# The RWKV-7 state update: old state added by identity products in PSUM, one scaling for each direction

## The chip, the cores and the metric

The kernel runs on one core of one Trainium2 chip. The metric is the device time of one execution in microseconds (us). Beside the timed executions, one execution was recorded by the hardware profiler; the profile's durations are those of that execution.

## The reference, cut to what matters

The model has two blocks. The change touches the first layer of the second block, whose core is a recurrence over tokens with a state of 64x64 for each of 12 heads, run once forward and once backward over 256 context tokens and 512 others:

```python
def rwkv7_scan(r, w, k, v, kk, bb, s0, reverse):
    def step(s, inp):
        r_t, w_t, k_t, v_t, kk_t, b_t = inp
        sa = jnp.einsum('bhij,bhj->bhi', s, kk_t)
        s = s * w_t[:, :, None, :] - sa[..., None] * b_t[:, :, None, :] + v_t[..., None] * k_t[:, :, None, :]
        return s, jnp.einsum('bhij,bhj->bhi', s, r_t)
    ...
    s, ys = lax.scan(step, s0, xs, reverse=reverse)
    return s, jnp.moveaxis(ys, 0, 1)
...
    for d in range(2):
        ...
        s_ctx, yc = rwkv7_scan(*tc[:6], zeros, d == 1)
        _, yl = rwkv7_scan(*tl[:6], s_ctx, d == 1)
```

Everything is in 32-bit floats. What comes before and after the recurrence (projections, gates, norms, the other layers and the whole first block) is the same before and after the change.

## The kernel before

**Chunks.** The kernel doesn't walk token by token. It cuts the 768 tokens into 12 chunks of 64, takes the heads in 6 pairs of two, and the chunks in 3 groups of 4. For each pair and group a good deal of work that doesn't depend on the state is done ahead: the decays and scaled keys (`inner_first`, called prep), the products between the tokens of a chunk (`products`, `keys_by_token`, called system), and the inverse of a triangular system for each chunk (`inner_rest`, `inner_second`, called inverse). What depends on the state is `Program.chain`, which runs 18 times (6 pairs by 3 groups), with 4 steps each. A step s handles chunk s of the forward direction (d = 0) and chunk 3-s of the backward one (d = 1).

**One step of the chain.** The state tile S has 128 partitions (two heads of 64), and 128 columns for each direction, in which the two heads stand as the diagonal 64x64 blocks; the other blocks are zero. S comes from a ring of five tiles that are zeroed once. In a step

- L1822 (two TensorE matmuls, one for each direction) adds WT times S to the PSUM tile u;
- the halves of u are copied, scaled, to VU: the forward half by ScalarE (the line in `chain` calls the helper `act`, so the profile shows it as L322), the backward half by VectorE (L1829);
- ScalarE scales the old state by the decay of the whole chunk, gs = gc * S, with two instructions of 128x128 (profile: L322, gs<-S,gc). The tile gs has one buffer, and EC, a tile of the inverse (L1763, written at L1765), has the same tag and so the same buffer;
- L1843 (four matmuls of 64x64, a head and a direction each) writes the step's new part to the PSUM tile sp, which has one buffer;
- L1851 (four VectorE instructions of 64x64) makes the new state: gc * sp + gs, block by block. At the first step of a pair there is no old state, and L1849 scales alone.

The last step of the last group has no update, so that 66 steps update the state, 60 of them with an old state. The new state is read by the next step's L1822 and, later, by the matmuls of L1864, which add its part to the outputs.

**What runs beside it.** `weave` (L1489) takes generators in turns: the chain of one group, the inverse of the next, the system of the one after that and the prep of the third, and, at a set rate, pieces of the projections (L363 to L365, three passes with weights and activations split in two parts; the profile calls their output acc). A `yield` in `chain` ends its turn. A scheduler orders the instructions of each engine when the program is built; an engine then runs its own list strictly in order, and semaphores hold it where an operand or a buffer isn't ready. TensorE's instructions of 32-bit operands appear in the trace as two passes for each matmul.

Of the kernel before, what the change touches and what calls it, by code (L numbers as in the profile page):

```python
# [11 lines left out]
F32 = mybir.dt.float32  # L12
F32R = mybir.dt.float32r
I32 = mybir.dt.int32
AF = mybir.ActivationFunctionType
ALU = mybir.AluOpType
PSUM = bass.MemoryType.PSUM

P = 128
# [254 lines left out]
class Program:  # L274
# [1013 lines left out]
    def rwkv(self, hl, hc):  # L1288
# [3 lines left out]
        with tc.tile_pool(name="rk", bufs=1) as rp:  # L1292
# [99 lines left out]
            inner = [{} for _ in range(nq)]  # L1392
            prep = lambda q: self.inner_first(q % 3, pairs[q // 3], inner[q]) if q < nq else iter(())
            system = lambda q: chain(self.products(q % 3, inner[q]), self.keys_by_token(inner[q])) if q < nq else iter(())
            inverse = lambda q: chain(self.inner_rest(q % 3, pairs[q // 3], inner[q]), self.inner_second(inner[q])) if q < nq else iter(())
            run(prep(0))
            run(system(0), prep(1))
# [3 lines left out]
            for q in range(nq):  # L1401
# [3 lines left out]
                if g == 0:  # L1405
                    if m:
                        feed.need((m - 1, "gate"))
                    run(self.pair_end(m - 1, pairs[m - 1]) if m else iter(()), system(q + 2), rate=RATE)
                    if m:
                        allow(m, "gate")  # L1410
                    start = ()
                    if m + 1 < NH2:
                        feed.need((m + 1, "v"))
                        start = self.pair_start(m + 1, pairs[m + 1])
                        feed.need((m + 1, "r"))
                    gens.append(chain(start, prep(q + 3)))
                else:
                    gens += [system(q + 2), prep(q + 3)]
# [273 lines left out]
    def inner_rest(self, g, pr, st):  # L1692
# [34 lines left out]
        for e in range(2):  # L1727
            H = half(1 - e)
            self.act(self.LB[H].rearrange("p (a j) t -> p a j t", j=2), st["system"](e))
        T = st["T"] = rp.tile([P, 8, 64], F32, tag="T", name="T")  # L1730
        for k in (1, 0):
            for e in range(2):
                H = half(1 - e)
                nc.sync.dma_start(out=T[H] if k else self.DB[H], in_=td[k, e::2, :4096].rearrange("u (s t) -> s u t", t=64))
        yield
# [5 lines left out]
    def inner_second(self, st):  # L1741
# [11 lines left out]
        def product(lhs, rhs, m=64, r0=0):  # L1753

            ps = self.psum("c", (P, 8, 32))
            for x in range(8):
                for i in (1, 0):
                    nc.tensor.matmul(ps[64 * i + r0:64 * i + r0 + m, x, :], lhs(x, half(i)), rhs(x, half(i)), start=True, stop=True)  # L1758
            return ps
# [3 lines left out]
        E, EC = self.E[0], rp.tile([P, 8, 32], F32, tag="gs", name="EC")  # L1763
        ps = product(lambda x, H: LB[H, x, :], lambda x, H: c16(Tm[H, x:x + 1], 0)[:, 0])
        tt(out=EC, in0=ps, in1=self.k_lmask.unsqueeze(1).to_broadcast([P, 8, 32]), op=ALU.mult)  # L1765
        self.act(c16(E, 0), b2(EC))
        yield
        ps = product(lambda x, H: Dm[H, x, :], lambda x, H: EC[H, x, :])
        tt(out=c16(Tm, 0), in0=c16(Tm, 0), in1=b2(ps), op=ALU.subtract)
# [28 lines left out]
    def chain(self, g, st, pr):  # L1798


        nc, rp = self.nc, self.rp
        tt = nc.vector.tensor_tensor
        half = lambda i: slice(64 * i, 64 * i + 64)
        Dm, VU, gc, M = self.DB, st["VU"], st["gc"], st["M"]
        if g == 0:
            self.state = None
            pr["y"] = rp.tile([P, 6, P], F32, tag="y", name="y")
        y = pr["y"]
        u = self.psum("u", (P, 2, 2, P))
        for d, h, j, e in self.units():  # L1810
            R = half(1 - e)
            nc.tensor.matmul(u[R, d, j, half(h)], Dm[R, 4 * d + 2 * h + j, :], st["akv"][R, 2 * d + h, j * 64:j * 64 + 64],
                             start=(d + h + j == 0), stop=True, skip_group_check=True)
        states = []
        for s in range(4):
            cs = (s, 3 - s)
            S = self.state
            states.append(S)
            if S is not None:
                for d in range(2):  # L1820
                    j, e = divmod(cs[d], 2)
                    nc.tensor.matmul(u[half(1 - e), d, j, :], st["WT"][:, d, j, half(1 - e)], S[:, d, :], start=False, stop=True, skip_group_check=True)  # L1822
            for d in range(2):
                j, e = divmod(cs[d], 2)
                O = half(1 - e)
                if d == 0:
                    self.act(VU[O, d, cs[d], :], u[O, d, j, :], scale=-0.5)
                else:
                    nc.vector.tensor_scalar(out=VU[O, d, cs[d], :], in0=u[O, d, j, :], scalar1=-0.5, scalar2=None, op0=ALU.mult)  # L1829
            if g == 2 and s == 3:  # L1830
                break
            nxt = self.S[self.turn % len(self.S)]
            self.turn += 1

            if S is not None:
                gs = rp.tile([P, 2, P], F32, tag="gs", name="gs")
                for d in range(2):
                    self.act(gs[:, d, :], S[:, d, :], AF.Copy, scale=gc[:, d, cs[d]:cs[d] + 1])
            yield
            sp = self.psum("sp", (P, 2, 64))  # L1840
            for d in range(2):
                for h in range(2):
                    nc.tensor.matmul(sp[half(h), d, :], st["bkT"][d][:, cs[d], half(h)], VU[:, d, cs[d], half(h)], start=True, stop=True)  # L1843
            for h in range(2):
                H = half(h)
                for d in range(2):
                    gd = gc[H, d, cs[d]:cs[d] + 1]
                    if S is None:
                        nc.vector.tensor_scalar(out=nxt[H, d, H], in0=sp[H, d], scalar1=gd, scalar2=None, op0=ALU.mult)  # L1849
                    else:  # L1850
                        nc.vector.scalar_tensor_tensor(out=nxt[H, d, H], in0=sp[H, d], scalar=gd, in1=gs[H, d, H], op0=ALU.mult, op1=ALU.add)  # L1851
            self.state = nxt
            yield
        yield
        ps = self.psum("misc", (P, 4, P))

        last = None
        for s, h, d in ((s, h, d) for s in range(4) for h in range(3) for d in (1, 0)):
            c = s if d == 0 else 3 - s
            X = half(c % 2)  # L1860
            if h < 2:
                ins = nc.tensor.matmul(ps[X, s, half(h)], M[:, d, h, c, half(1 - c % 2)], VU[:, d, c, half(h)], start=(s == 0 and h == 0), stop=True, skip_group_check=True)
            elif states[s] is not None:
                ins = nc.tensor.matmul(ps[X, s, :], st["AR"][d][:, c // 2, 3 - 3 * (c % 2), :], states[s][:, d, :], start=False, stop=True, skip_group_check=True)  # L1864
            else:
                continue
            last = self.queue(ins, last)
        for d in range(2):
            t0 = FIRST[g][d] // 2
            for e in range(2):  # L1870
                X = half(e)

                src = ps[X, e::2, :] if d == 0 else ps[X, (3 - e)::-2, :]
                dst = y[X, t0:t0 + 2, :]
                if g == 0:

                    i, s = (0, e) if d == 0 else (1, 1 - e)
                    nc.vector.tensor_copy(y[X, i, :], ps[X, s, :])
                elif g == 1:
                    nc.vector.tensor_copy(dst, src)  # L1880
                else:
                    tt(out=dst, in0=dst, in1=src, op=ALU.add)
        if g == 0:
            for d in range(2):
                for e in range(2):
                    X = half(e)
                    i, s = (1, e + 2) if d == 0 else (0, 3 - e)
                    tt(out=y[X, i, :], in0=y[X, i, :], in1=ps[X, s, :], op=ALU.add)
        yield
# [331 lines left out]
```

## Time and profile before

| | us |
|---|---|
| median of 3 runs | 2346.11 (2336.16 to 2348.5) |
| profiled execution, its own time | 2352.9 |
| span of the profiled execution | 2351.1 |
| TensorE matmul busy | 2187.3 (93%) |
| VectorE busy | 1623.3 (69%) |
| ScalarE busy | 1077.8 (46%) |
| GpSimd busy | 337.3 (14%) |

The recurrence and what is woven with it fill the stretch from about 1270 to 1885 us of the span. A share of busy time is a mean over a stretch; it doesn't say by itself which engine ends last. The profile has views for that: the busy time of each engine in short stretches, the chain of work that ended last (followed back from the end, from each instruction to what released it), and the waits of each engine by what ended them. In the rows PE is TensorE, PEld its weight load, DVE VectorE, ACT ScalarE, POOL GpSimd; PEclk is the clock that TensorE was granted, as a share of full speed.

### The profile page before, as it was taken

How to read it: one execution, taken by the hardware profiler on the slowest of the kernel's cores; microseconds unless marked ns; L12 is line 12 of the kernel's file. 1: busy time of each engine (PE TensorE's matmuls, PEld its weight loads, DVE VectorE, ACT ScalarE, POOL GpSimd, SP SyncE). 2: the span in 40 equal slices, each digit the busy share in tenths (PEclk: the TensorE clock that was granted, in tenths of full speed). 3: DMA queues.
4: the chain of work that ended last, by engine and by line, in shares of the span. 5: the costliest groups of instructions: out<-in, count | busy, mean ns of one | idle time of the engine just before them, and what ended most of it. 6: DMA issues, size and time to landing. Idle time of an engine off the chain costs nothing. (4 is left out here: it accounts for less than half of the span.)

```text
span 2351.1 us, 40197 instructions
## 1 busy us (share of the span) xinstructions
PE 2187.3 (93%) x15774; PEld 1752.6 (75%) x15774; DVE 1623.3 (69%) x3014; ACT 1077.8 (46%) x2033; POOL 337.3 (14%) x722
## 2 busy tenths in 40 slices
PE   6889989999998999999898999999899999999996
PEld 4667768878775788888676677777677777888885
DVE  6799886568859787444675868787866556555544
ACT  3466353223335332333564545556554355655542
POOL 1321020000002000000004232332413100000001
PEclk9999999999999999999998979999998999999998
DMA  8433356566624656323322222212212242422211
GB/s 290 138 127 127 134 158 194 179 208 194 195 74 125 210 183 208 100 87 101 134 77 64 53 58 47 68 40 67 54 46 57 85 158 100 131 72 72 72 55 45
DMA packets 203742, 269.66 MB, mean 115 GB/s; under 512 B 125216, under 2 KB 137376, under 8 KB 203168
## 3 DMA queue, kind: packets, MB, share of 16 engines
q1 hardware_dynamic: 203552, 267.09, 37.3%
q8 instruction: 124, 2.03, 0.3%
q14 instruction: 66, 0.54, 0.1%
HBM read 250.38 MB, written 16.66 MB: 114 GB/s over the span
## 5 line engine op out<-in xcount | busy, mean ns | idle before, releaser
L363 PE MATMUL acc<-hh,wh 128*128 128x512 f32 x1416 | 574.9, 407 | 36.3 <-ACT wh L322 21.0
L365 PE MATMUL acc<-hh,wl 128*128 128x512 f32 x1416 | 571.9, 404 | 7.9 <-POOL wl L340 4.2
L364 PE MATMUL acc<-hl,wh 128*128 128x512 f32 x1416 | 572.7, 404 | 1.3 <-DVE hl L340 1.2
L322 ACT ACTIVATE wh<-ws 128x1024 fp32r<-128x1024 f32 (+4 forms) x307 | 275.8, 902 | 423.8 <-PE acc L364 313.4
L340 DVE TENSOR_TENSOR wl<-ws,wh 128x1024 fp32r<-128x1024 f32 (+3 forms) x294 | 305.3, 1041 | 202.6 <-ACT wh L322 193.7
L363 PEld LDWEIGHTS acc<-hh,wh 128*128 128x128 f32 x1416 | 271.4, 192 | 98.3 <-ACT wh L322 23.0
L365 PEld LDWEIGHTS acc<-hh,wl 128*128 128x128 f32 x1416 | 270.7, 191 | 74.6 <-DVE wl L340 8.4
L364 PEld LDWEIGHTS acc<-hl,wh 128*128 128x128 f32 x1416 | 271.6, 192 | 60.2 <-issue 5.7
L447 DVE SCALAR_TENSOR_TENSOR ws<-ws,cact 128x1024 f32<-128x1024 f32 x144 | 180.2, 1254 | 83.5 <-DMA ws<-in_ada_dram 82.3
L365 PE MATMUL acc<-gh,wl 128*128 128x512 f32 x352 | 137.9, 392 | 3.2 <-DVE wl L340 3.2
L363 PE MATMUL acc<-gh,wh 128*128 128x512 f32 x352 | 137.9, 392 | 2.2 <-ACT gh L322 2.2
L364 PE MATMUL acc<-gl,wh 128*128 128x512 f32 x352 | 138.0, 392 | 0.6 <-DVE gl L340 0.6
L322 ACT ACTIVATE a<-a 128x512 f32<-128x512 f32 x44 | 27.8, 633 | 188.4 <-DVE a L988 188.2
L1671 POOL TENSOR_TENSOR sO<-sN,sX 64x15 f32<-64x15 f32 (+2 forms) x270 | 79.7, 295 | 154.6 <-DMA sN<-lt 134.9
L1672 POOL TENSOR_TENSOR sX<-sX,sO 64x15 f32<-64x15 f32 (+2 forms) x270 | 85.1, 315 | 21.1
L2024 POOL TENSOR_TENSOR raw<-raw,k_axial 128x512 f32<-128x512 f32 x16 | 21.9, 1367 | 413.1 <-ACT raw L322 413.1
L365 PEld LDWEIGHTS acc<-gh,wl 128*128 128x128 f32 x352 | 66.5, 189 | 18.2 <-DVE wl L340 4.4
L363 PEld LDWEIGHTS acc<-gh,wh 128*128 128x128 f32 x352 | 66.4, 189 | 16.7 <-ACT gh L322 3.1
L364 PEld LDWEIGHTS acc<-gl,wh 128*128 128x128 f32 x352 | 66.5, 189 | 15.1 <-DVE gl L340 1.2
L447 DVE SCALAR_TENSOR_TENSOR ada<-ws,cact 128x1024 f32<-128x1024 f32 x48 | 58.6, 1221 | 26.5 <-DMA ws<-in_ada_dram 26.5
L1851 DVE SCALAR_TENSOR_TENSOR S<-sp,gc,gs 64x64 f32<-64x64 f32 x240 | 58.4, 280 | 20.4 <-PE sp L1843 18.7
L363 PE MATMUL acc<-hc,wh 128*128 128x256 f32 x208 | 64.3, 309 | 4.3 <-ACT wh L322 3.7
(581 smaller groups left out, 4328.4 us busy)
## 6 DMA issues: line engine op xcount, KB each, us to landing
ws<-in_ada_dram SPq DMA_DIRECT2D x144, 512.0 KB, 4.3
ws<-in_up_dram SPq DMA_DIRECT2D x88, 512.0 KB, 4.1
ws<-in_od_in_dram SPq DMA_DIRECT2D x44, 512.0 KB, 3.5
ws<-in_ev_in_dram SPq DMA_DIRECT2D x60, 256.0 KB, 2.9
ws<-in_down_dram SPq DMA_DIRECT2D x32, 384.0 KB, 3.1
ws<-in_w_in_dram SPq DMA_DIRECT2D x22, 512.0 KB, 4.5
ws<-in_down_dram SPq DMA_DIRECT2D x32, 320.0 KB, 2.9
ws<-in_ev_in_dram SPq DMA_DIRECT2D x18, 512.0 KB, 3.5
```

The source lines that it names most:

```text
L322: ins = self.nc.scalar.activation(out=out, in_=in_, func=func, **k)
L340: (engine or self.nc.vector).tensor_tensor(out=lo, in0=x, in1=hi.bitcast(F32), op=ALU.subtract)
L363: nc.tensor.matmul(ps, wh[:, s], xh, start=start, stop=False)
L364: nc.tensor.matmul(ps, wh[:, s], xl, start=False, stop=False)
L365: nc.tensor.matmul(ps, wl[:, s], xh, start=False, stop=stop)
L447: nc.vector.scalar_tensor_tensor(out=w, in0=ws, scalar=1.0, in1=c, op0=ALU.mult, op1=ALU.mult, accum_out=d[:, m:m + 1])
L1671: pt(out=ob, in0=N[:, :j, j:j + 1].to_broadcast(sh), in1=X[:, j:j + 1, j:].to_broadcast(sh), op=ALU.mult)
L1672: pt(out=X[:, :j, j:], in0=X[:, :j, j:], in1=ob, op=ALU.subtract)
L1851: nc.vector.scalar_tensor_tensor(out=nxt[H, d, H], in0=sp[H, d], scalar=gd, in1=gs[H, d, H], op0=ALU.mult, op1=ALU.add)
L2024: nc.gpsimd.tensor_tensor(out=raw, in0=raw, in1=self.k_axial[:, 0, :], op=ALU.mult)
```

## The change

The scaling of the old state on ScalarE, and with it the tile gs, goes away; EC has that buffer for itself. Instead the old state enters the sum in PSUM: two products of a 128x64 half of an identity matrix (`k_ident`) with the whole of S (256 columns, both directions) write S to sp, and the four matmuls add to it. sp is now 128 columns wide for each direction, so that it holds whole state tiles, zero blocks included. One instruction for each direction then scales sp by gc and writes the new state: VectorE for the forward one, ScalarE for the backward one. The first step of a pair (no old state) works as before. The identity products stand ahead of the `yield`, where the scaling of gs stood.

```diff
@@ -1832,23 +1832,24 @@
             nxt = self.S[self.turn % len(self.S)]
             self.turn += 1
 
+            sp = self.psum("sp", (P, 2, P))
             if S is not None:
-                gs = rp.tile([P, 2, P], F32, tag="gs", name="gs")
-                for d in range(2):
-                    self.act(gs[:, d, :], S[:, d, :], AF.Copy, scale=gc[:, d, cs[d]:cs[d] + 1])
+                for h in (1, 0):
+                    nc.tensor.matmul(sp[half(h)], self.k_ident[:, half(h)], S, start=True, stop=False, skip_group_check=True)
             yield
-            sp = self.psum("sp", (P, 2, 64))
             for d in range(2):
                 for h in range(2):
-                    nc.tensor.matmul(sp[half(h), d, :], st["bkT"][d][:, cs[d], half(h)], VU[:, d, cs[d], half(h)], start=True, stop=True)
-            for h in range(2):
-                H = half(h)
-                for d in range(2):
-                    gd = gc[H, d, cs[d]:cs[d] + 1]
-                    if S is None:
-                        nc.vector.tensor_scalar(out=nxt[H, d, H], in0=sp[H, d], scalar1=gd, scalar2=None, op0=ALU.mult)
-                    else:
-                        nc.vector.scalar_tensor_tensor(out=nxt[H, d, H], in0=sp[H, d], scalar=gd, in1=gs[H, d, H], op0=ALU.mult, op1=ALU.add)
+                    nc.tensor.matmul(sp[half(h), d, half(h)], st["bkT"][d][:, cs[d], half(h)], VU[:, d, cs[d], half(h)], start=S is None, stop=True, skip_group_check=True)
+            for d in range(2):
+                gd = gc[:, d, cs[d]:cs[d] + 1]
+                if S is None:
+                    for h in range(2):
+                        H = half(h)
+                        nc.vector.tensor_scalar(out=nxt[H, d, H], in0=sp[H, d, H], scalar1=gd[H], scalar2=None, op0=ALU.mult)
+                elif d == 0:
+                    nc.vector.tensor_scalar(out=nxt[:, d, :], in0=sp[:, d, :], scalar1=gd, scalar2=None, op0=ALU.mult)
+                else:
+                    self.act(nxt[:, d, :], sp[:, d, :], AF.Copy, scale=gd)
             self.state = nxt
             yield
         yield
```

In the lists below an instruction's name stands with its output, its operands and its shape (partitions by columns), and x2 for two such rows in a row. Behind the edit the lines of the changed kernel have other numbers: L1843 is now L1842, L1851 is L1850 and, for ScalarE, L322.

TensorE, third step of a chain in the middle of the run, before; acc are projections, c products of the inverse:

```order
L1822 MATMUL u<-S_8515,WT 64x128 x2
L363 MATMUL acc_13713<-hh,wh 128x512
L364 MATMUL acc_13713<-hl,wh 128x512
L365 MATMUL acc_13713<-hh,wl 128x512
L1843 MATMUL sp<-VU,bkT_11537 64x64
L1758 MATMUL c<-EC,DB 64x32 x16
L1843 MATMUL sp<-VU,bkT_11537 64x64
L1843 MATMUL sp<-VU,bkT_11579 64x64 x2
```

The same step after:

```order
L1822 MATMUL u<-S_8515,WT 64x128 x2
L1838 MATMUL sp<-S_8515,k_ident 64x256 x2
L1842 MATMUL sp<-VU,bkT_11492 64x64 x2
L1585 MATMUL c<-wl,lw_8507 128x256
L1842 MATMUL sp<-VU,bkT_11531 64x64 x2
L1585 MATMUL misc<-wl,lw_8507 128x256
L1585 MATMUL c<-al,lw_8508 128x256
L1585 MATMUL misc<-al,lw_8508 128x256
L1758 MATMUL c<-DB,E_8506 32x32 x16
L1838 MATMUL sp<-S_8511,k_ident 64x256 x2
```

The identity products of the step follow u directly, where three projection matmuls stood; those of the step behind it (S_8511) stand ahead of its u.

ScalarE around one state update of another chain, before; a wait on DVE_49 is one on VectorE, PE_49 on TensorE; exc, lw and inc belong to prep, arT and bkT to the system:

```order
L322 ACTIVATE exc<-exc 128x256 [waits DVE_49]
L322 ACTIVATE lw<-inc 128x256
L322 ACTIVATE inc<-inc 128x256 [waits Activation_49]
L322 ACTIVATE gc<-lw 128x4
L322 ACTIVATE gs<-S_8511,gc 128x128 [waits DVE_49]
L322 ACTIVATE gs<-S_8511,gc 128x128
L322 ACTIVATE VU<-u 64x128 [waits PE_49]
L322 ACTIVATE arT<-c 128x512 [waits PE_49]
```

The same place after:

```order
L322 ACTIVATE exc<-exc 128x256 [waits DVE_49]
L322 ACTIVATE lw<-inc 128x256
L322 ACTIVATE S_8511<-sp,gc 128x128 [waits DVE_49]
L322 ACTIVATE inc<-inc 128x256 [waits Activation_49]
L322 ACTIVATE gc<-lw 128x4
L322 ACTIVATE VU<-u 64x128 [waits PE_49]
L322 ACTIVATE arT<-c 128x512 [waits PE_49]
```

The two scalings of the old state have gone, and the write of the new backward state has come in, with a wait on VectorE. In all 60 steps that wait is for the forward scaling of the same step, which reads the same PSUM tile; ScalarE's list has 1814 entries before and 1751 after.

## Rows read from the trace of the kernel before

**Rows 1.** Stretches, whole recurrence stage: us, busy us of PE, PEld, DVE, ACT, POOL (instructions), PEclk, DMA share, GB/s

```profile
1270.00:1885.00 615.00, 575.39 (x7825) 446.94 (x7825) 448.81 (x1119) 314.94 (x733) 186.00 (x559) 0.92 0.25 57
```

**Rows 2.** The same view, one head pair cut where the bound changes

```profile
1496.50:1522.20 25.70, 25.70 (x350) 19.65 (x352) 17.04 (x42) 16.41 (x35) 9.18 (x30) 1.00 0.23 55
1522.20:1538.40 16.20, 15.04 (x198) 11.00 (x198) 15.52 (x45) 10.34 (x30) 0.88 (x2) 1.00 0.15 35
1538.40:1550.00 11.60, 9.13 (x215) 7.56 (x215) 10.26 (x28) 7.43 (x19) 2.69 (x9) 0.98 0.17 30
1550.00:1558.30 8.30, 8.19 (x103) 6.56 (x104) 7.41 (x16) 0.93 (x4) 6.58 (x23) 0.62 0.01 2
1558.30:1565.00 6.70, 6.46 (x95) 4.94 (x95) 5.85 (x17) 5.57 (x16) 1.91 (x5) 1.00 0.51 102
1565.00:1578.00 13.00, 13.00 (x233) 10.68 (x234) 9.88 (x27) 7.46 (x16) 3.99 (x13) 1.00 0.33 68
1578.00:1594.00 16.00, 11.89 (x141) 8.99 (x142) 14.81 (x26) 7.37 (x12) 9.37 (x23) 0.89 0.30 58
1594.00:1602.20 8.20, 8.20 (x36) 6.70 (x36) 3.82 (x9) 3.87 (x8) 2.75 (x10) 0.80 0.64 161
```

**Rows 3.** Chain of waits, 1270 to 1890 us: share of 620 us by line

```profile
by line: PE c L1758 11.4%; PE acc L363 8.6%; PE acc L365 7.8%; PE acc L364 7.8%; issue 3.5%; PE sp L1843 3.4%; PE u L1822 3.0%; PE c L1649 2.8%; DVE m L1653 2.6%; PE c L1686 2.3%; PE misc L1862 2.2%; DVE S L1851 2.2%; ACT L322 1.9%; DMA T<-
```

**Rows 4.** The same chain, pieces within the pair: start, us, what

```profile
1529.96 0.38 DVE S L1851 x2
...
1530.35 0.49 DVE S L1851 x2
...
1544.38 0.41 ACT gs L322
...
1544.81 0.28 DVE S L1851
```

**Rows 5.** Groups of the stage: line, engine, names, shapes, count | busy us, mean ns | idle before, releasers

```profile
L1851 DVE SCALAR_TENSOR_TENSOR S<-sp,gc,gs 64x64 f32<-64x64 f32 x240 | 58.4, 280 | 20.4 <-PE sp L1843 18.7
...
L322 ACT ACTIVATE gs<-S,gc 128x128 f32<-128x128 f32 x120 | 42.2, 393 | 52.5 <-DVE S L1851 39.6 <-PE c L1758 10.8 <-DVE S L1849 1.5
...
L322 ACT ACT_TABLE_LOAD x20 | 25.7, 1283 | 0.3
...
L322 ACT ACTIVATE inc<-inc 128x256 f32<-128x256 f32 x30 | 12.4, 414 | 0.7
```

**Rows 6.** Waits of the stage: engine, line, waited for: us, times, longest

```profile
DVE VU L1829 <- ACT VU L322: 28.3, 28, 2.6
...
ACT gs L322 <- PE c L1758: 10.8, 9, 1.7
```

**Rows 7.** Timeline of one step with little beside it: start, us, instructions [idle before]

```profile
1705.92 0.27 ACT L322 ACTIVATE VU<-u 64x128 f32<-64x128 f32 x1 [0.60 <-PE u L1822]
...
1706.22 0.28 DVE L1829 TENSOR_SCALAR VU<-u 64x128 f32<-64x128 f32 x1 [2.56 <-ACT VU L322]
...
1707.09 0.98 DVE L1851 SCALAR_TENSOR_TENSOR S<-sp,gc,gs 64x64 f32<-64x64 f32 x4 [0.58 <-PE sp L1843]
```

**Rows 8.** Groups of one instruction with 128x128 from PSUM, in the later layer

```profile
L2092 DVE COPY R<-misc 128x128 f32<-128x128 f32 x16 | 4.7, 292 | 9.3 <-PE misc L2090 8.9
```

**Rows 9.** The same view, ScalarE, a column's scale for each partition

```profile
L322 ACT ACTIVATE kcf<-misc,kx 128x128 f32<-128x128 f32 x16 | 5.9, 368 | 0.0
```

**Rows 10.** Timeline of TensorE, products with S: start, us, passes

```profile
1521.34 0.39 PE L1864 MATMUL misc<-S,ar 128*64 128x128 f32 x4
1521.57 0.40 PE L1862 MATMUL misc<-VU,m 128*64 128x64 f32 x8
```

**Rows 11.** Timeline of TensorE, products that fill the array, 256 columns

```profile
1865.20 1.89 PE L1523 MATMUL c<-E,k 128*128 128x256 f32 x8
```

## The prediction

> **What bounds the kernel now.** I read the stage first, then one pair of heads by stretches, then the chain of waits. In the whole recurrence stage TensorE is busy 575.4 of 615 us, VectorE 448.8 (73%), ScalarE 314.9 (51%) [rows 1]. So TensorE is the nominal bound, and all its idle time is 39.6 us. Within one pair (105.7 us) two kinds of stretch alternate [rows 2]. In the first, sixth and last stretch TensorE is busy all the time (25.70, 13.00 and 8.20 us), and in the fourth 8.19 of 8.30 at a granted clock of 0.62: together 55.2 us. In the other four, 50.5 us, VectorE is the busier engine or close to it (15.52 of 16.2, 10.26 of 11.6, 5.85 of 6.7, 14.81 of 16) and TensorE waits for parts of the time. The chain of waits then says what of the state update lies on the path: over 620 us the four VectorE instructions of L1851 hold 2.2%, 13.6 us [rows 3], though VectorE spends 58.4 us on them [rows 5]. Three quarters of that work is already under something else, mostly TensorE.
>
> **What goes: VectorE.** The four instructions of a step take 0.98 us back to back [rows 7]. One 128x128 read from PSUM takes VectorE 0.29 us [rows 8]. A step loses 0.69 us of VectorE, 60 steps 41.4. Only what is on the path counts: 13.6 us become 13.6 x 0.29/0.98 = 4.0, a gain of **9.6 us**. This holds where the next thing on VectorE's list is the work of prep, as in the second stretch, where pieces of L1851 of 0.38 and 0.49 us stand on the chain [rows 4]. Where instead the next step's u waits for the state, both directions are needed. Then 0.98 becomes 0.29 + 0.03 + 0.37 = 0.69 a step, since the backward scaling follows the forward one: 0.37 is ScalarE's 128x128 from PSUM with a column as scale [rows 9], and 0.03 the handover from one engine to the other on the tile u (0.27 us from 1705.92, next start 1706.22) [rows 7]. If all of the chain's share were of that kind, the gain would be 13.6 x (0.98 - 0.69)/0.98 = 4.0 us, the low end of this term.
>
> **Whether the two directions run side by side.** They read the same PSUM tile, and the changed program holds the backward one until the forward one is done. The kernel before has the same pattern at u: VectorE waits 28 times, 28.3 us in all, for ScalarE's copy [rows 6]. I take them one after the other. The Trainium skill, "PSUM — Partial Sum Buffer", section "PSUM bank collisions raise a hardware error", says that two engines must not be in the same bank and the same quarter of the partitions at one time, reads included; the wait at u agrees. It also speaks against the change's split, which the skill's "TensorEngine Tiling (Array Packing)", section "PSUM Bottleneck", would advise (use both engines to empty PSUM). Side by side, a step would cost 0.37 us instead of 0.69, which on the 14 steps' worth that the chain holds (13.6/0.98) would be 4.5 us more gain; by the wait, none.
>
> **What goes: ScalarE.** Two scalings of 0.393 us (42.2 us over 120) leave [rows 5], and one of 0.37 comes: some 20 us of ScalarE, which is not the bound. The scaling of the old state had time, from one update to the next. The one place on the chain in this pair is 0.41 us, where gs had stood behind the products of the inverse that read EC from the same buffer [rows 4]; in the stage such waits are 10.8 us in 9 places [rows 6]. With one such piece a pair it would be 6 x 0.41 = 2.5 us; VectorE and TensorE have other work there, so I take **1 us** of gain, between 0 and 2.5.
>
> **What comes: TensorE.** Two identity products a step, each two passes of 256 columns by a 128x64 operand. The nearest row is the products of L1864, the same 128x64 shape with 128 columns: four passes, in two halves of the array, take 0.23 us from their start to that of the next group (1521.34 to 1521.57) [rows 10]. Twice the columns: 0.46 us a step, 27.6 for 60. If the halves didn't overlap, the row for products that fill the array holds: eight passes of 256 columns in 1.89 us, or 0.94 for four, 57 in all [rows 11]. I take 0.46, since the shape is the same, and keep 0.94 for the range. Where does it lie? In the order of the changed kernel they follow u directly, or are pulled ahead; of the ten of a pair I place four in the first, all-TensorE stretch, by the instructions around them, and six in stretches where TensorE waits for VectorE or for VU. A wait hides them there: after u, TensorE needs both halves of VU, 0.27 + 0.03 + 0.28 us [rows 7], and 0.46 fits into that. If that cover is filled with projections, as before the change, they cost their full price. So 24 of 60 are exposed: 24 x 0.46 = **11.0 us** lost, between 0 and 27.6 (57 without overlap). The four accumulating products have the count and columns of those before: nothing. EC's own buffer costs nothing in time.
>
> **What is late next.** VectorE's gap in the second and fifth stretch closes to TensorE: there TensorE is busy 15.04 of 16.2 and 6.46 of 6.7 us [rows 2], and the identity products take some of the rest. So a VectorE gain larger than that gap is not to be had there.
>
> **The sum.** Against the profiled execution: 2352.9 - 9.6 - 1.0 + 11.0 = 2353.3. That execution lies 6.8 us above the median, 2346.1, so the forecast for a median is 2346.1 + 0.4 = **2346.5 us**, no change. A measurement of this kernel can tell about 0.5%, 11.7 us, from no change.
>
> **Rival 1, faster: VectorE's relief counts in all its stretches.** If the six steps of ten that fall in VectorE's stretches each shorten the path by the full 0.69 us, 36 x 0.69 = 24.8 us go; with 1.0 for gs and 11.0 for the exposed products the sum is -14.8, 2331 us. With all products under waits it is -25.8, 2320. It decides from (11.7 + 10.0)/0.69 = 31 steps on the path. For it: VectorE at 87 to 96% of those stretches. Against it: the chain holds 14 steps' worth, and TensorE is nearly as busy in two of the four.
>
> **Rival 2, slower: the identity products stand in TensorE's way.** TensorE has 39.6 us of idle time in the whole stage, and not all of it is where a state is ready. If all 60 are exposed, it costs 27.6 - 10.6 = +17, 2363 us; at 0.94 each, +46, 2392. At the clock of 0.62 in the fourth stretch [rows 2] a product is dearer by 1/0.62. It decides when exposed time passes 11.7 + 10.6 = 22.3 us: 48 steps at 0.46, or 24 at 0.94. For it: 93.6% of the stage is TensorE. Against it: in the order the products replace projections in the wait for VU.
>
> **Rival 3, slower: the backward state stands in ScalarE's queue.** The write of the backward state now is on the recurrence, in a list that is served in order, behind pieces of prep of 0.41 us or a table load of 1.28 us [rows 5], and everything behind it on ScalarE waits for VectorE's scaling: inc, gc and the next VU. With a table load ahead in two steps of ten and a piece of 0.41 in four, the delay is 0.42 us a step, 25 us in all if every step were on the path: +25, 2372. It decides from 0.19 us a step on the path (11.3/60). For it: VectorE never had that delay in L1851. Against it: TensorE works through projections while the chain waits, in half of the time.
>
> **How the numbers follow.** Forecast 0.43, rival 1 0.27, rival 2 0.18, rival 3 0.12. The bounds of the forecast's own terms are -4.0 to -9.6, 0 to -2.5 and 0 to +27.6, which is -12 to +24 around no change; its own range is 2335 to 2358. Faster by over 0.5% has rival 1, 0.27; slower has rivals 2 and 3, 0.30. To leave no more than 2 in 10 out, the range goes down to 2322, short of rival 1's end, and up to 2374, over rival 2 at 0.46 and rival 3, but not to the case without overlap.
>
> **What would show it.** L1850 and the ScalarE write should take 0.29 and 0.37 us, and the write should begin some 0.03 us behind the end of L1850; a start at the same time breaks that step. Busy time of VectorE in the stage should fall by 41, of ScalarE by 20, and of TensorE's matmuls rise by about 28. L1850 should hold some 4 us of the chain; the identity products should stand there with 11. If they hold more than 22, rival 2 is right; if waits of u or of L1864 for the ScalarE write sum to over 11 us, rival 3; if the VectorE stretches shrink by over 3 us a pair, rival 1. If the stage keeps its length and the time changes by more than 12 us, the cause lies outside the recurrence, and the prediction's basis is wrong.

## The result, and the profile after

The changed kernel took 2374.84 us (median of 4 runs, 2365.07 to 2391.8) against 2347.31 of the kernel before beside it: ratio 1.013, 95% interval 1.0089 to 1.0171. Six more runs of it, told below, gave 1.0144 (1.0108 to 1.0181). It is slower, by 28 to 36 us from median to median. The forecast was no change, 2346.5 us, with 2322 to 2374 as range. Two runs told below, one of `half_id` (3525 us) and one of a second set of the kernel before (2370 us), were disturbed and are left out of the ratios and means; medians are over all runs.

The stage of the recurrence by itself, from the first to the last of VectorE's writes of VU (the columns are those of [rows 1]), in the changed kernel:

```profile
1283.30:1905.00 621.70, 582.85 (x7987) 453.84 (x7989) 400.92 (x933) 294.50 (x670) 193.44 (x558) 0.93 0.24 56
```

and in a second profile of the kernel before:

```profile
1269.10:1868.40 599.30, 558.16 (x7747) 432.15 (x7749) 445.64 (x1113) 314.63 (x730) 189.72 (x560) 0.94 0.26 59
```

The relief came as forecast: VectorE 45 us less, ScalarE 20 less. TensorE rose by 25, and its idle time stayed at 39 to 41 us. The stage is 22 us longer than in that profile, and 12 longer than in the first one of the kernel before, whose line stands further down. The groups of the update in the changed kernel, which answer to [rows 5]:

```profile
L1838 PE MATMUL sp<-S,k_ident 128*64 128x256 f32 x240 | 41.5, 398 | 0.0
...
L322 ACT ACTIVATE S<-sp,gc 128x128 f32<-128x128 f32 x60 | 21.9, 364 | 45.1 <-DVE S L1850 44.4
L1850 DVE TENSOR_SCALAR S<-sp,gc 128x128 f32<-128x128 f32 x60 | 20.9, 349 | 26.1 <-PE sp L1842 25.7
L1829 DVE TENSOR_SCALAR VU<-u 64x128 f32<-64x128 f32 x72 | 20.5, 285 | 28.6 <-ACT VU L322 15.7 <-POOL sO L1671 9.2 <-POOL sX L1672 2.4
```

One scaling takes VectorE 0.349 us and ScalarE 0.364. A step in the timeline, to set beside [rows 7]: TensorE first, then the two writes of the state.

```profile
1546.67 0.44 PE L1822 MATMUL u<-S,WT 128*64 128x128 f32 x4
1546.94 0.60 PE L1838 MATMUL sp<-S,k_ident 128*64 128x256 f32 x4
1547.47 1.12 PE L1758 MATMUL c<-EC,DB 64*64 64x32 f32 x32
...
1549.02 0.35 DVE L1850 TENSOR_SCALAR S<-sp,gc 128x128 f32<-128x128 f32 x1
1549.41 0.37 ACT L322 ACTIVATE S<-sp,gc 128x128 f32<-128x128 f32 x1 [0.42 <-DVE S L1850]
```

From the start of the identity products to the next product it is 0.53 us, and TensorE never stands idle ahead of them (the 0.0 in their line). The backward write begins 0.04 us behind the end of the forward one: one after the other, not side by side.

**Reading the time and the clock apart.** Each run comes with the mean clock that TensorE was granted. In ten runs of the changed kernel the times spread by 27 us (2365 to 2392), but time x clock by 9 (2282 to 2292), and by 2 in the first four. So I split each time into time x clock ("at full clock") and the rest ("lost to the clock"). It is a way to read, not an exact law, since waiting for a transfer doesn't stretch with the clock. Means over runs, the standard error of the time in brackets:

| kernel | runs | time | at full clock | lost to the clock |
|---|---|---|---|---|
| before (all that ran beside the others) | 79 | 2345.6 (0.9) | 2263.2 | 82.5 |
| changed | 10 | 2379.6 (2.7) | 2286.3 | 93.3 |

The 34 us are 23 at full clock and 11 from the clock. The profile's stage is read alike, length times PEclk: 621.7 x 0.93 = 578 in the changed kernel, 599.3 x 0.94 = 563 in the one before. PEclk has two digits, so such a number is good to some 3 us.

### The profile page after: what moved, and what is told of

Read it like the earlier page. It is cut to its first block, busy times and chain, and to the rows that moved or that the text cites. A ratio compares the mean times of both kernels' runs of the same rounds, so it can differ in the third digit from the quotient of the medians.

```text
span 2371.8 us, 40402 instructions
## 1 busy us (share of the span) xinstructions
PE 2204.4 (93%) x16014; PEld 1766.5 (74%) x16014; DVE 1578.2 (67%) x2834; ACT 1056.9 (45%) x1973; POOL 345.1 (15%) x722
## 5 line engine op out<-in xcount | busy, mean ns | idle before, releaser
L322 ACT ACTIVATE wh<-ws 128x1024 fp32r<-128x1024 f32 (+4 forms) x307 | 275.7, 901 | 421.1 <-PE acc L364 319.5
L322 ACT ACTIVATE a<-a 128x512 f32<-128x512 f32 x44 | 27.8, 633 | 208.8 <-DVE a L988 208.6
L1671 POOL TENSOR_TENSOR sO<-sN,sX 64x15 f32<-64x15 f32 (+2 forms) x270 | 86.1, 319 | 171.3 <-DMA sN<-lt 151.5
L1672 POOL TENSOR_TENSOR sX<-sX,sO 64x15 f32<-64x15 f32 (+2 forms) x270 | 85.5, 317 | 21.0
L2175 PEld LDWEIGHTS acc<-hc,ws 128*128 128x128 f32 x288 | 55.2, 192 | 14.4 <-issue 5.3
```

The costliest lines, as they stand in the source:

```text
L322: ins = self.nc.scalar.activation(out=out, in_=in_, func=func, **k)
L1671: pt(out=ob, in0=N[:, :j, j:j + 1].to_broadcast(sh), in1=X[:, j:j + 1, j:].to_broadcast(sh), op=ALU.mult)
L1672: pt(out=X[:, :j, j:], in0=X[:, :j, j:], in1=ob, op=ALU.subtract)
L2175: p.nc.tensor.matmul(q, pan[:, k % pk * P:k % pk * P + P], x[0][:, k, :], start=(k == 0), stop=(k == nk - 1))
```

## The experiments

Three theories stood at the start: the identity products' own time on TensorE (A), the backward state in ScalarE's queue (B), and the other order that the scheduler gives the whole stage (C). A fourth (D) came up on the way.

**Leave the identity products out.** (`no_id`) sp is one tile, zeroed once; the old state isn't added.

```diff
-                for h in (1, 0):
-                    nc.tensor.matmul(sp[half(h)], self.k_ident[:, half(h)], S, start=True, stop=False, skip_group_check=True)
...
-..., VU[:, d, cs[d], half(h)], start=S is None, stop=True, skip_group_check=True)
+..., VU[:, d, cs[d], half(h)], start=True, stop=True, skip_group_check=True)
```

> The changed kernel without its identity products: sp is one tile, zeroed once, the four products start it anew, and the two scalings stand as changed. The old state is left out of the update. Theory A (the identity products stand on TensorE's path, at 0.43 to 0.58 us each from their start to the next instruction, 60 times, and VectorE's relief gives little back): the 26 to 33 us that the change costs go away, 2340 to 2350 us. Theory B (the backward state's write in ScalarE's queue holds the recurrence): it is still there, 2365 us or more. Theory C (the new order of the instructions costs, whatever they are): no forecast, but more likely above 2355.

Measured: 2377.39 us, ratio 1.0129 (1.0078 to 1.0179). By the time alone A fell and B stood.

**Add them to the kernel before, without use.** (`before_dead_id`)

```diff
+            sp = self.psum("sp", (P, 2, P))
             if S is not None:
+                for h in (1, 0):
+                    nc.tensor.matmul(sp[half(h)], self.k_ident[:, half(h)], S, start=True, stop=False, skip_group_check=True)
                 gs = rp.tile([P, 2, P], F32, tag="gs", name="gs")
```

> The kernel before with the identity products added where the change has them, in a sp tile of 128 columns a direction; the four products then write over them, so they have no use, and the old scaling and the four VectorE instructions stay. Theory A: 60 pairs at 0.43 to 0.58 us on the path, 2370 to 2382 us. Theory B: within 6 us of the kernel before, 2341 to 2353. Theory C: between the two.

Measured: 2372.9 us, ratio 1.0127 (1.0094 to 1.0159), in A's range. Its stage:

```profile
1273.40:1898.00 624.60, 589.34 (x7987) 457.62 (x7989) 446.64 (x1113) 315.01 (x730) 195.58 (x558) 0.93 0.24 57
```

That is 624.6 x 0.93 = 581, 18 above the 563 of the kernel before, with VectorE and ScalarE as busy as there.

**Half of the columns.** (`half_id`)

```diff
-                    nc.tensor.matmul(sp[half(h)], self.k_ident[:, half(h)], S, ...)
+                    nc.tensor.matmul(sp[half(h), :, half(h)], self.k_ident[:, half(h)], S[:, :, half(h)], ...)
```

> The changed kernel with identity products of half the size: each moves only the 64 columns a direction of its own head, 128 in place of 256, into one sp tile that was zeroed once. The result is the same. Theory A: half of the columns' 0.43 us a step goes, 13 us less than the changed kernel, 2355 to 2367 us. Theory B: as the changed kernel, 2370 to 2380.

Measured: 2385.83 us, ratio 1.0163 (1.0123 to 1.0203), not faster than the changed kernel; by the time A's forecast failed. Its profile isn't read here.

**Both scalings on VectorE.** (`both_vector`)

```diff
-                elif d == 0:
+                else:
                     nc.vector.tensor_scalar(out=nxt[:, d, :], in0=sp[:, d, :], scalar1=gd, scalar2=None, op0=ALU.mult)
-                else:
-                    self.act(nxt[:, d, :], sp[:, d, :], AF.Copy, scale=gd)
```

> The changed kernel with both scalings on VectorE, so that the state no longer passes through ScalarE's queue. Theory A: within 6 us of the changed kernel, 2369 to 2381, since VectorE is not what ends last and gets back only 21 of the 41 us that it was relieved of. Theory B: the cost goes away, 2345 to 2360.

Measured: 2372.32 us, ratio 1.0125 (1.0093 to 1.0157): in A's range, not in B's. Taken together the four don't fit one theory by their times: adding the products alone costs what the change costs, and the change without them costs it too. Split by the clock they do:

| kernel | runs | time | at full clock | lost to the clock |
|---|---|---|---|---|
| no_id | 6 | 2373.2 (5.0) | 2256.0 | 117.1 |
| before_dead_id | 6 | 2373.2 (1.8) | 2288.6 | 84.7 |
| half_id | 5 | 2381.8 (3.5) | 2279.8 | 102.0 |
| both_vector | 6 | 2372.9 (1.6) | 2289.8 | 83.1 |

Whatever has the products needs some 25 us more at full clock, half of the columns 17, where half of the price would be 12 or 13: the price seems not to go by the columns alone. The kernel without them needs none, 7 less than the one before, but loses 35 us more to the clock.

**TensorE's order of before.** A table with the place of each matmul in TensorE's list of the kernel before is laid over the changed kernel; its other engines stay with the scheduler. (`after_pe_order`, and the same for `no_id_pe_order`)

```diff
+def as_before(tc):
+    ...
+    for i, j in zip(whole, whole[1:]):
+        tc.add_manual_dep(j, i.name, NOSYNC, reason="order")
```

> The changed kernel with TensorE's list in the order of the kernel before, word for word; the identity products of a step stand directly behind the second matmul of u of that step. The other engines' lists are left to the scheduler. Theory A (the identity products' own time on TensorE costs): still 2365 to 2380 us. Theory C (the cost is the other order that the scheduler gives the recurrence stage): 2340 to 2358 us. If both hold, halfway, 2358 to 2365.

> The kernel without identity products (two scalings in place of four instructions and the old scaling, the old state left out of the update) with TensorE's list in the order of the kernel before; it has the same matmuls as that one. In its own order it took as long as the changed kernel. Theory C: at or below the kernel before, 2325 to 2347 us. Theory B (the backward state's write in ScalarE's queue holds the recurrence): 2360 us or more in this order too.

Measured: 2366.39 us, ratio 1.0104 (1.0053 to 1.0155), and 2372.21 us, ratio 1.0123 (1.0064 to 1.0183). At full clock 2290.8 and 2259.5, lost 77.2 and 110.0. So C is no explanation of the price: in the old order the identity products cost their 28 us at full clock. The order sets part of the clock's share, 16 us less lost in the old order. One wait of TensorE's goes the same way, the one for T, a tile of the inverse that comes through memory. In the kernel before, the changed kernel and the changed kernel in the old order (columns as in [rows 6]):

```profile
PE c L1758 <- DMA T<-td: 4.9, 5, 1.4
```

```profile
PE c L1758 <- DMA T<-td: 15.0, 10, 2.6
```

```profile
PE c L1758 <- DMA T<-td: 3.4, 4, 1.2
```

So the changed kernel's 39 us of idle time aren't the 41 of the one before: what it waited for VectorE's VU, DB and E (16 to 19 us in the two profiles of that one) has shrunk to 7, and 10 us of waiting for T have come. In the kernel with the old order the chain of waits covers the whole stage (that of the changed kernel, in its own order, only a part), and shows the products with 3.2% of 612 us, 20 us, where the prediction had 11 (and rival 2 asked for more than 22):

```profile
by line: PE c L1758 11.2%; PE acc L363 8.5%; PE acc L364 8.0%; PE acc L365 7.6%; issue 4.1%; PE sp L1843 3.5%; PE u L1822 3.3%; PE sp L1838 3.2%; POOL sX L1672 2.4%; PE c L1649 2.4%; ACT L322 2.2%; POOL sO L1671 2.2%; PE misc L1864 2.1%; PE
```

**VectorE's relief without TensorE's burden.** (`two_fused_pe_order`) Two VectorE instructions of 128x128 in place of four of 64x64 on the kernel before, with the old scaling kept:

```diff
-                        nc.vector.scalar_tensor_tensor(out=nxt[H, d, H], in0=sp[H, d], scalar=gd, in1=gs[H, d, H], op0=ALU.mult, op1=ALU.add)
+                    nc.vector.scalar_tensor_tensor(out=nxt[:, d, :], in0=sp[:, d, :], scalar=gd, in1=gs[:, d, :], op0=ALU.mult, op1=ALU.add)
```

> The kernel before with one VectorE instruction of 128x128 a direction in place of two of 64x64 (sp is one tile whose other blocks were zeroed once), everything else as it was, and TensorE's list in the order of the kernel before. VectorE loses about 0.29 us a step, 17 us in all. By what the chain of waits of the kernel before holds of those instructions (13.6 us) some 4 us faster, 2335 to 2347 us; by theory A, B and C alike not slower.

> The kernel before, unchanged, for a second profile of it: how far two profiles of one program lie apart, ahead of the recurrence stage and in it. All theories: 2340 to 2350 us, ahead of the stage within 3 us of the first profile if the 3 to 10 us that four other kernels lie behind there, with the same instructions in the same order, are the kernels' own, and as far behind as those if they are scatter.

Measured: 2340.88 us, ratio 0.999 (0.9954 to 1.0025), and the unchanged kernel 2340.34, ratio 0.9994 (0.9964 to 1.0024). VectorE's stage time falls from 446 to 416 us, and the time doesn't follow: 2259.2 at full clock, 84.8 lost. Its stage, and that in the first profile of the kernel before:

```profile
1274.60:1867.30 592.70, 549.64 (x7747) 428.13 (x7749) 416.25 (x982) 314.48 (x730) 192.63 (x560) 0.95 0.26 60
```

```profile
1272.80:1882.30 609.50, 570.03 (x7747) 442.25 (x7749) 446.03 (x1115) 314.27 (x730) 185.92 (x558) 0.92 0.25 57
```

With two fused instructions the stage is 592.7 x 0.95 = 563. The second profile of the kernel before lies some 4 us ahead of the first at the stage's start, and its stage is 10 us shorter: 599.3 x 0.94 = 563 and 609.5 x 0.92 = 561, so the difference between the two is the clock's.

**Where the clock falls without the products.** Stretches in `no_id_pe_order`, around the third step of a pair's last chain:

```profile
1547.60:1551.00 3.40, 3.32 (x42) 2.56 (x37) 3.37 (x9) 1.77 (x7) 0.42 (x2) 1.00 0.21 24
1551.00:1554.40 3.40, 1.95 (x19) 1.31 (x19) 1.05 (x4) 1.94 (x4) 0.00 (x0) 1.00 0.80 179
1554.40:1557.80 3.40, 3.40 (x44) 3.00 (x46) 1.65 (x4) 0.61 (x2) 0.00 (x0) 0.51 0.41 93
1557.80:1581.70 23.90, 23.90 (x238) 18.30 (x237) 11.79 (x25) 7.67 (x17) 10.85 (x35) 0.50 0.18 35
```

and the same place in `two_fused_pe_order`, which has the same list of matmuls:

```profile
1550.20:1553.70 3.50, 3.32 (x45) 2.52 (x42) 3.44 (x10) 2.79 (x8) 0.42 (x2) 1.00 0.42 64
1553.70:1557.10 3.40, 3.24 (x47) 2.52 (x47) 2.09 (x7) 1.68 (x3) 0.00 (x0) 1.00 0.76 173
1557.10:1560.50 3.40, 3.40 (x71) 2.73 (x69) 2.60 (x8) 1.78 (x5) 0.00 (x0) 1.00 0.40 102
```

In the first TensorE is busy for 1.95 of 3.40 us while the transfers run at 0.80, then the clock is 0.50 for 27 us although TensorE is busy all of that time. In the second it is busy for 3.24 and keeps 1.00. What TensorE waits for is in the waits of the second stretch of `no_id_pe_order`:

```profile
PE c L1760 <- DMA T<-td: 1.5, 2, 1.1
...
PEld c L1760 <- ACT kd L322: 1.2, 1, 1.2
```

In the stretches of `two_fused_pe_order` there is no wait for T. T is what GpSimd's elimination makes (L1671, L1672) and what comes back through memory. Hence theory D: relieved engines bring TensorE earlier to a tile that isn't there; it then stands in one piece, and the clock falls.

**Cut the elimination short.** (`no_id_short_pool`, `before_short_pool`; TensorE's order as before)

```diff
-        for j in range(15, 0, -1):
+        for j in range(15, 8, -1):
```

> The kernel without identity products, TensorE's list in the order of the kernel before, with 7 of the 15 levels of GpSimd's elimination left (L1671 and L1672; the rest of the inverse's first part is left out, as is the old state). Theory D (with VectorE and ScalarE relieved, TensorE comes earlier to the tiles T and DB that GpSimd makes and that pass through memory, stands there in one piece, and the clock falls behind that): the loss to the clock falls from 110 to 80 us or less, and the time to 2330 to 2345 us. Theory B (the backward state on ScalarE): loss still 105 to 117, 2360 us or more.

> The kernel before with 7 of the 15 levels of GpSimd's elimination left (the rest is left out), as a control for the run without identity products. Theory D: less to gain than there, 2330 to 2344 us, and at most 10 us less lost to the clock. Theory B: as the kernel before.

Measured: 2320.03 us, ratio 0.9892 (0.9852 to 0.9932), and 2320.86 us, ratio 0.9892 (0.9859 to 0.9925). Lost to the clock: 64.0 and 63.6. Taking the wait away gives the kernel without products 51 us and the kernel before 26, of which 46 and 19 are the clock's; D had allowed the latter 10. GpSimd's tiles are late in the kernel before too, so a late tile alone doesn't make the 28 us by which the two differ in the loss; but with the tiles early that difference is gone, so the late tile is needed for it. VectorE is as busy as before (443.9 us in the stage), so it isn't VectorE that gained from a shorter GpSimd. And with the tiles early, the kernel relieved on VectorE and ScalarE is as fast as the one that isn't (2254.2 and 2256.2 at full clock): the relief is worth 2 us.

**ScalarE's part.** (`no_id_both_vector`: the edit of `both_vector` on `no_id_pe_order`), and a control for the data (`before_drop_state`: all work as before, L1851 without the old state):

```diff
-                    if S is None:
+                    if True:
                         nc.vector.tensor_scalar(out=nxt[H, d, H], in0=sp[H, d], scalar1=gd, scalar2=None, op0=ALU.mult)
```

> The kernel without identity products, TensorE's list in the order of the kernel before, with both scalings on VectorE (the old state is left out). Theory B: the loss to the clock falls from 110 to about 82 us, the time to 2340 to 2348 us. Theory D: still 100 us or more, 2360 to 2375 us.

> The kernel before with its four VectorE instructions scaling the new part alone; ScalarE still scales the old state, which then goes nowhere (the old state is left out). TensorE's list in the order of the kernel before. All work is there, only the data differ. Theory B and D: 2340 to 2350 us, 75 to 90 us lost to the clock. If the data set the clock: 105 us or more lost, 2365 us or more.

Measured: 2349.23 us, ratio 1.0041 (1.0006 to 1.0076), and 2351.12 us, ratio 1.0021 (0.9991 to 1.0051). Lost to the clock: 92.5 and 86.6; at full clock 2261.3 and 2264.4. So the data of the state update don't set the clock. Of the 28 us that `no_id_pe_order` loses beyond the kernel before, 17 go when the backward state leaves ScalarE: B has a part, and it acts through the clock, not at full clock. With 92.5 the run lies between what B and D had forecast (82, and 100 or more).

**The products where GpSimd holds nothing up.** (`after_short_pool`: the short elimination in `after_pe_order`)

> The changed kernel with TensorE's list in the order of the kernel before and 7 of the 15 levels of GpSimd's elimination (the rest is left out). If the identity products always cost their time on TensorE: 24 to 30 us above the kernel before with the same 7 levels, 2344 to 2350 us, all of it at full clock (time x clock 2280 to 2286). If it was the wait for GpSimd that left them no room: 2320 to 2332 us.

Measured: 2340.55 us, ratio 0.997 (0.994 to 1.0). Against `before_short_pool` that is 21 us more in the mean, a little less than forecast, and 2282.1 against 2256.2 at full clock, 25.9 more. Their stages, first with the products, then without:

```profile
1276.10:1872.40 596.30, 564.27 (x7987) 432.95 (x7989) 402.23 (x934) 296.06 (x670) 110.17 (x302) 0.97 0.25 58
```

```profile
1269.90:1851.00 581.10, 544.03 (x7749) 421.47 (x7750) 443.94 (x1114) 314.50 (x730) 114.04 (x302) 0.97 0.26 60
```

At one clock, TensorE's busy time and the stage's length grow by 20 and 15 us. So some 5 us lie in waits (TensorE's idle time goes from 37 to 32 us), and three quarters don't hide when the wait for GpSimd is gone either.

**Twice as many products, and the changed kernel once more.**

```diff
-                for h in (1, 0):
+                for h in (1, 0, 1, 0):
```

> The changed kernel with each identity product issued twice (the second pair writes the same values again), 60 pairs more. If a pair costs its whole time on TensorE: time x clock rises by 25 to 30 us over the changed kernel's 2286, to 2311 to 2316, and the time to 2392 to 2408 us. If the second pair finds room in waits: under 2300 at full clock, 2370 to 2385 us.

> The changed kernel, unchanged, on the chip of the run beside it, for more of its times: 2286 us at full clock as in its first four, and 83 to 95 us lost to the clock, 2370 to 2380 us.

Measured: 2370.73 us, ratio 1.011 (1.007 to 1.015), and 2381.37 us, ratio 1.0144 (1.0108 to 1.0181). At full clock 2297.3 and 2286.7; lost 74.5 and 94.9. A was wrong on the whole time: the kernel with twice the products isn't slower. At full clock the second set costs 11 us, not the 25 to 30 of a full price; by the forecast alone (under 2300) it would have found room in waits. In the stage alone the price shows:

```profile
1259.60:1895.70 636.10, 593.10 (x8227) 455.01 (x8228) 404.28 (x934) 295.50 (x670) 192.96 (x560) 0.95 0.24 56
```

636.1 x 0.95 = 604, against 578 and 580 (624.1 x 0.93) in the two profiles of the changed kernel: 25 us for the second set. But its stage starts 24 to 27 us earlier than in those, of which some 15 fall in the first 1090 us, where the lists are the same instruction for instruction; and it loses 20 us less to the clock. The profile thus puts what is missing between 25 and 11 ahead of the stage; why the work there was faster is not shown.

**The elimination shared with VectorE.** (`split_elim`; `two_fused_split` joins it with the two instructions of 128x128)

```diff
+            pt = (nc.gpsimd if j > 8 else nc.vector).tensor_tensor
             ob = o[:, :j, :16 - j]
```

> The kernel before with the last 8 of the 15 levels of the elimination on VectorE in place of GpSimd, TensorE's list as before; the result is the same. With 8 levels left out it was 25 us faster. If VectorE's 16 short instructions a group (256 in all, by rows of 64x64 on it at most 0.28 us each) find room: 2322 to 2338 us; if VectorE then ends last, 2340 to 2360.

> The same split of the elimination, with the state update in two VectorE instructions of 128x128 in place of four of 64x64 (no identity products), TensorE's list as before; the result is the same. VectorE has 17 us less to do than in the run with the split alone: 2318 to 2334 us, and not slower than that run.

Measured: 2418.97 us, ratio 1.0285 (1.0226 to 1.0345), and 2406.46 us, ratio 1.0249 (1.0186 to 1.0312). VectorE, whose list is served in order, now stands waiting for GpSimd's first half, 40.4 us in 12 places, and TensorE's idle time in the stage doubles to 80 us (664.8 less 584.6). No version here with the same result beats the kernel before.

## Why the prediction was wrong

**TensorE's term, 11.0 us: mis-sized.** The unit price was a little low: 0.46 forecast, 0.43 to 0.62 from start to next start, 0.52 in the mean of the 47 steps whose products stand together at a granted clock of 1.00. The step that failed is that six of ten products lie in waits. Length times PEclk of the stage is 560 to 569 us in nine profiles of eight kernels without the products (those with the shared elimination left aside), 578 to 587 in six profiles of five kernels with them, 604 with twice as many: 18 us for the first set and 23 to 25 for the second, of 27.6 on paper (31 at 0.52). TensorE's idle time was nearly the same with and without them: 39 and 41 us in the two profiles shown first, 37 and 41 in the mean of the six and of the nine, so waits hid some 4 us, where the prediction hid 16.6. I read it so, from the two orders of TensorE's list: a wait at a place isn't room if the list behind it is full, for when the products fill the wait behind u, the projections that stood there are only moved to another place, where they cost what they cost. The prediction said so, as the price if that cover is gone, and then took the cover for granted.

**VectorE's term, 9.6 us: not there.** VectorE lost the forecast time, and the four kernels that have this relief in whole or part, no products and the whole elimination are at 563 to 566 us in the stage at full clock, where the kernel before is at 561 and 563. Over the whole time they are 2 to 7 us below it at full clock (2256.0 to 2261.3 against 2263.2), no more than the differences ahead of the stage told below. The wait of L1850 for sp even grew from 18.7 us [rows 5] to 25.7 in fewer instructions: VectorE comes earlier and waits longer. The prediction read the 2.2% of L1851 on the chain as time that goes when the work goes [rows 3]. The share did go: of the 13.6 us less than 1 is left on the chain of the changed kernel with TensorE's old order. What was late next was named as TensorE; GpSimd's elimination, at 14% busy, was not named at all, and cutting it short took 26 us from the kernel before, 19 of them the clock's.

**The clock: not in the sum.** 11 of the 34 us. In the changed kernel the loss is 93 us, with both scalings on VectorE 83, with TensorE's old order 77. So the order and ScalarE's share of the write set it, but each difference is only some three to five times its standard error of 3 us, and no single place explains it. The wait for T fits in part: 15.0 and 16.4 us in the two profiles of the changed kernel, 4.9 and 4.8 in those of the one before, 3.4 in the old order; but it is 11.4 with both scalings on VectorE, where the loss is that of the kernel before. In the trace the backward write starts 0.03 us behind the end of the forward one in the median, and 17 of 60 are held over 0.1 us in ScalarE's list, up to 1.29, 6.7 us in all: rival 3's delay is real, and smaller than the 25 us that it was given. By the prediction's own sign rival 3 fails: waits of u and of the products for the outputs for ScalarE's write come to 0.2 us in the stage, not 11.

**The single steps.** That the two directions don't run side by side held, 0.04 us between them. It is what the Trainium skill, "PSUM — Partial Sum Buffer", section "PSUM bank collisions raise a hardware error", asks of two engines on one bank in the same partitions, reads included; both writes read the tile sp. ScalarE's 0.37 held (0.364); VectorE's 0.29, taken from a copy, was 0.349. The gs term of 1 us can't be told from nothing. Rival 2 comes nearest, by mechanism and by 2363 us; it lacked the clock, and it kept 10.6 us of gain that weren't there. Without that gain and with its 27.6 it would have said 2374, which is near the 2374.84 measured by luck: 11 us of the measured loss are the clock's and some 5 lie ahead of the stage.

**What stays open.** The 11 us of the clock are only in part explained. Of the 23 us at full clock some 18 are in the stage, and those are the products'. The rest lies ahead of it, in work that didn't change: there the changed kernel's 4500th matmul starts at 1086.4 and 1087.0 us in two profiles, that of the kernel before at 1080.6 and 1078.4, that of the kernel with twice the products at 1071.5. The two programs with two profiles keep their places to some 2 us, with the same list of instructions up to there; why is not shown.

## What to carry to other kernels

Moving work from a half-idle engine to the one that is 93% busy costs its time on that engine, even where the trace shows waits at the very place: ask whether the list behind the wait has anything to give up. A share of the chain is time that an engine ended last, not time to be had; before it is booked as a gain, name the next thing that is late on every other engine, GpSimd and transfers included, and price it by cutting that short. Split runs by the granted clock before comparing parts: here three kernels with quite different work took the same time, because the one that did less lost more to the clock. And an idle time that stays the same can be made of other waits than before: compare the waits by what ended them.

## What was not expected of the hardware

In `no_id_pe_order` TensorE stood for 1.45 us between 1551.0 and 1554.4, and then the granted clock was 0.50, the lower of its two levels, for 27 us while TensorE was busy throughout. And doing more matmuls (the second set of products, 25 us of the stage) left the whole time 8 us below the changed kernel's mean (standard error 3), with 19 us less lost to the clock.
